# The opening of a two-layer encoder: the first quarter's scale and shift split into two eighths, the first weight items run chunk by chunk

## The chip, the cores and the metric

The kernel runs on one core of one Trainium2 chip. The metric is the device time in microseconds; lower is better. Engines are TensorE (PE, its weight loads PEld), VectorE (DVE), ScalarE (ACT), GpSimd (POOL) and SyncE (SP), whose queue issues nearly all DMAs.

## The reference, cut to what matters

```python
def hybrid_layer(x, c, ...):
    mod = jax.nn.silu(c) @ ada_w + ada_b                      # 1024 -> 6 x 1024
    sh_m, sc_m, g_m, sh_f, sc_f, g_f = jnp.split(mod, 6)
    h = rms_norm(x, norm_mix_g) * (1 + sc_m) + sh_m           # 256 tokens x 1024
    proj = h @ w_in
    ...                                                       # three attention branches, merge, FFN
```

Two such layers follow one another, then a last RMSNorm. All is float32. At the start of the program `h` of layer 0 needs two of the six modulation vectors, the shift `sh_m` and the scale `sc_m`; each is a row of 1024 numbers, a product of the vector silu(c) with a 1024 x 1024 matrix.

## The kernel before, in words

Tokens are two tiles of 128 (t = 0, 1). The model width of 1024 is eight chunks of 128 (kc = 0 to 7). A float32 product is made of three passes in a faster format: an operand is split into a rounded part (`hi`, by a cast on ACT) and the remainder (`lo`, by a subtraction on DVE), and the products are hi x hi, lo(weight) x hi and hi(weight) x lo.

Weights come in items of up to 256 rows x 512 columns, that is two chunks of the contraction. `load_split` (L242 to L254) loads an item into `raw`, casts it into `whi` (L189) and makes `wlo` (L190). The function `mm` of an item (L263 to L272) issues for one token tile the three passes over its two chunks: 6 matmuls, so 12 for both tiles. An item's eight-chunk sum takes four items.

The first 12 items belong to three groups of columns (416, 512 and 512 wide) whose items are interleaved, so that items 0, 1 and 2 need only chunks 0 and 1 of `h`, items 3, 4, 5 chunks 2 and 3, and so on. Item 2 is loaded in two DMAs, items 0 and 1 in one. Accordingly the scale and shift are made in four quarters of 256 columns each (two chunks):

- `first_loads(q)` (L861) issues the quarter's 8 DMAs of 256 KB, rows of 256 numbers. Nothing but SP's order and a limit of 8 DMAs in flight holds them up.
- `first_sums(q)` (L877) multiplies them with silu(c) on PE (L883, a 32-column weight), 8 matmuls of 512 columns, and ACT copies the sums out (L886).
- `first_mod(q)` (L889) transposes them on PE (L892), DVE reduces them (L894), and `first_apply` (L898) makes scale and shift (L902, L905, L903), then the two chunks of `h`: `hi` on ACT (L910), the full value on DVE (L911) and `lo` (L915).

The main loop (L929 on) writes the order of PE by hand for the opening: 16 warm-up matmuls (L842), the transposes of the normalised x (`first_x`), the first quarter, then item 0; the sums of the next quarter before the second of three items, its transposes before the third. The order of SP's queue is that of the code: the columns of parameters, x, the constants (`con`, L83: rotary tables, mask and the 128 x 128 identity that transposes need, which is its last 128 columns), the first quarter, items 0 and 1, the second quarter, item 2 and so on. The parameters at item 7 (L320 to L334), and what comes behind, read the rest of the constants.

Of the kernel before, what the change touches and what calls it, by code (L numbers as in the profile page):

```python
# [36 lines left out]
def encoder_kernel(ctx: ExitStack, tc: tile.TileContext, x, consts, cols, rows, ada_b, rpb, ada_w, w_in,  # L37
                   w_uq, w_ukv, w_na, w_mla, w_gqa, w_out, w_gu, w_dn, fng, out):
    nc = tc.nc
# [30 lines left out]

    def tpb():
        return pstp.tile([P, 512], F32, tag="tp", name=nm("tp"))
# [41 lines left out]
    mods = {}  # L114
# [121 lines left out]
    items = []  # L236
    state = {}

    def add(srcs, nk, n, mm, post=None, pre=()):
        items.append(dict(srcs=srcs, nk=nk, n=n, mm=mm, post=post, pre=list(pre)))  # L240
        return items[-1]

    def load_split(it):
        nk, n = it["nk"], it["n"]
        raw = rawp.tile([P, 2, 512], F32, tag="raw", name=nm("raw"))
        c = 0
        for src in it["srcs"]:
            w = src.shape[1]
            nc.sync.dma_start(raw[:, 0:nk, c:c + w], src.rearrange("(k p) n -> p k n", p=P))
            c += w  # L250
        hi = spl.tile([P, 2, 512], F32R, tag="whi", name=nm("whi"))
        lo = spl.tile([P, 2, 512], F32R, tag="wlo", name=nm("wlo"))
        split_to(hi[:, 0:nk, 0:n], lo[:, 0:nk, 0:n], raw[:, 0:nk, 0:n])
        it["w"] = (hi, lo)  # L254

    def group(units_src, nkc, n, lhs, post, bank=None):

        ps = {}
        nu = (nkc + 1) // 2
# [27 lines left out]
    cur = [0]  # L287
# [545 lines left out]
    xT0 = {}  # L833
# [5 lines left out]
    def warm(n):  # L839

        for _ in range(n):
            nc.tensor.matmul(warm_ps, warm_w[:, 0:P], warm_w, start=True, stop=True)  # L842

    def last_pe():
        return next(i for i in reversed(nc.cur_bb.bb.instructions) if i.engine == mybir.EngineType.PE)

    def first_x():
        xT = act.tile([P, KC, S], F32, tag="lo", name=nm("xT"))
        for hf in range(2):
            xT0[hf] = xT[:, hf * 4:hf * 4 + 4, :]  # L850
        for t in range(NT):
            for hf in range(2):
                sumsq(t, hf, ss0[t])
            r = x_rstd(t, ss0[t])
            for hf in range(2):
                nc.scalar.copy(xT0[hf][:, :, t * P:(t + 1) * P], transposed(x_scaled(t, r, hf)))
        state[0]["hT"] = act_tiles()
        mods[(0, 1)] = modp.tile([P, KC], F32, tag="c1", name=nm("cm"))
        mods[(0, 0)] = modp.tile([P, KC], F32, tag="c0", name=nm("cm"))

    def first_loads(q):  # L861

        raws = []
        for v in range(4):
            raw = t4([P, 2, 2, 256])
            for mi, m in enumerate((1, 0)):
                c0 = m * D + q * 256
                nc.sync.dma_start(raw[:, :, mi, :], ada_w[0, v * 256:(v + 1) * 256, c0:c0 + 256].rearrange(
                    "(k p) n -> p k n", p=P))
            raws.append(raw.rearrange("p k m n -> p k (m n)"))  # L870
# [6 lines left out]
    def first_sums(q, raws):  # L877


        ps = tpb()  # L880
        for kc in range(KC):
            j = kc % 4
            nc.tensor.matmul(ps[32 * j:32 * j + 32, :], scz[:, kc, :], raws[kc // 2][:, kc % 2, :], start=(kc < 4),  # L883
                             stop=(kc >= 4), tile_position=(0, 32 * j))
        four = t2([P, 512])
        nc.scalar.copy(four, ps)  # L886
        return four

    def first_mod(q, four):  # L889
        pv = tpb().rearrange("p (j q) -> p j q", j=4)  # L890
        for j in range(4):
            nc.tensor.transpose(pv[:, j, :], four[:, j * P:(j + 1) * P], ident)  # L892
        red = sm(4)
        nc.vector.tensor_reduce(out=red, in_=pv.rearrange("p j (r z) -> p j r z", z=32)[:, :, :, 0], op=ALU.add, axis=AX.X)  # L894
        with tc.high_priority():
            first_apply(q, red)

    def first_apply(q, red):  # L898
        k0 = 2 * q
        A, B, hT = mods[(0, 1)], mods[(0, 0)], state[0]["hT"]  # L900
        r2 = sm(2)
        nc.vector.tensor_tensor(out=r2, in0=red[:, 0:2], in1=colp(0, "b", KC + k0, 2), op=ALU.add)  # L902
        nc.vector.scalar_tensor_tensor(out=A[:, k0:k0 + 2], in0=r2, scalar=1.0, in1=colp(0, "gm", k0, 2), op0=ALU.add,  # L903
                                       op1=ALU.mult)
        nc.vector.tensor_tensor(out=B[:, k0:k0 + 2], in0=red[:, 2:4], in1=colp(0, "b", k0, 2), op=ALU.add)  # L905
        full = t2([P, 2, S])
        for j in range(2):
            kc = k0 + j
            xv = xT0[q // 2][:, kc % 4, :]
            nc.scalar.activation(hT[0][:, kc, :], xv, AF.Identity, scale=A[:, kc:kc + 1], bias=B[:, kc:kc + 1])  # L910
            nc.vector.tensor_scalar(out=full[:, j, :], in0=xv, scalar1=A[:, kc:kc + 1], scalar2=B[:, kc:kc + 1],  # L911
                                    op0=ALU.mult, op1=ALU.add)
        for j in range(2):
            kc = k0 + j
            nc.vector.tensor_tensor(out=hT[1][:, kc, :], in0=full[:, j, :], in1=hT[0][:, kc, :].bitcast(F32),  # L915
                                    op=ALU.subtract)

    def run_mm(t, i):
        it = items[i]
# [4 lines left out]
    def step(t, i):  # L924
        run_due(cur[0])
        run_mm(t, i)
        cur[0] += 1

    pend = []  # L929
    for i, it in enumerate(items):  # L930
        if i in flush:
            while pend:
                step(1, pend.pop(0))
        if i == 0:
            raws = first_loads(0)
            with tc.manual_schedule(engines={mybir.EngineType.PE}):
                warm(16)
                first_x()
                four = first_sums(0, raws)
                warm(1)  # L940
                first_mod(0, four)
                warm(1)
        for f in side.get(i, ()):
            f()
        load_split(it)
        if i < 12:

            q1 = i // 3 + 1
            if i % 3 == 1 and q1 < 4:
                raws = first_loads(q1)  # L950
            with tc.issue_after(last_pe()), tc.manual_schedule(engines={mybir.EngineType.PE}):
                if i % 3 == 1 and q1 < 4:
                    four = first_sums(q1, raws)
                if i % 3 == 2 and q1 < 4:
                    first_mod(q1, four)
# [78 lines left out]
```

## Time and profile before

| | |
|---|---|
| median of 3 runs | 815.99 us (815.93 to 816.52) |
| the profiled execution | 816.62 us |
| its span, first to last instruction | 814.7 us |
| mean granted TensorE clock | 0.997 of full speed |
| busy | PE 97%, DVE 74%, ACT 56%, POOL 3% |
| DMA | 187 MB, mean 230 GB/s |

Times in the profile count from the first instruction. A matmul's busy time overlaps that of the next, since matmuls are pipelined; how far apart two of them start tells more. "Idle before" an instruction is time in which its engine did nothing, with the instruction that ended the wait. For a DMA the profile tells when SP issued it and how long after that it had landed.

### The profile page before, as it was taken

How to read it: one execution, taken by the hardware profiler on the slowest of the kernel's cores; microseconds unless marked ns; L12 is line 12 of the kernel's file. 1: busy time of each engine (PE TensorE's matmuls, PEld its weight loads, DVE VectorE, ACT ScalarE, POOL GpSimd, SP SyncE). 2: the span in 40 equal slices, each digit the busy share in tenths (PEclk: the TensorE clock that was granted, in tenths of full speed). 3: DMA queues.
4: the chain of work that ended last, by engine and by line, in shares of the span. 5: the costliest groups of instructions: out<-in, count | busy, mean ns of one | idle time of the engine just before them, and what ended most of it. 6: DMA issues, size and time to landing. Idle time of an engine off the chain costs nothing.

```text
span 814.7 us, 10812 instructions
## 1 busy us (share of the span) xinstructions
PE 791.9 (97%) x3778; PEld 630.9 (77%) x3778; DVE 599.2 (74%) x961; ACT 454.1 (56%) x788; POOL 24.6 (3%) x40
## 2 busy tenths in 40 slices
PE   7999999999999999999989999999999999999996
PEld 4677677788878878888878877777887888888884
DVE  3469899889777888865576798878987676665562
ACT  4465978645484444454466797764548544444441
POOL 1001000000000000000000020000000000000000
PEclk9999999999999999999999999999999999999998
DMA  9987598795548888875865568768765677765521
GB/s 313 360 281 202 169 308 280 259 312 192 192 159 293 292 284 318 275 261 185 206 191 173 173 192 281 231 220 294 229 205 181 222 243 223 255 219 182 183 102 52
DMA packets 113414, 187.20 MB, mean 230 GB/s; under 512 B 14672, under 2 KB 34256, under 8 KB 113360
## 3 DMA queue, kind: packets, MB, share of 16 engines
q1 hardware_dynamic: 113360, 186.51, 71.4%
q8 instruction: 30, 0.49, 0.2%
q14 instruction: 24, 0.20, 0.1%
HBM read 185.44 MB, written 1.05 MB: 229 GB/s over the span
## 4 chain that ended last, share of the span: by engine, by line
issue 49%; PE 31%; DVE 7%; ACT 6%; DMA 5%; POOL 1%; SPq 0%; POOLq 0%; DVEq 0%; ACTq 0%
PE mm L271 24%; DVE wlo L190 3%; DMA raw<-in_ada_w_dram 2%; PE tp L569 2%; DMA raw<-in_w_mla_dram 2%; DVE acc L142 1%; PE o L638 1%; ACT P L596 1%; PE tp L617 1%; ACT whi L189 1%; PE tp L883 1%; ACT tm L220 1%; DMA con<-in_consts_dram 1%; DMA s<-in_ada_w_dram 1%; ACT P L601 1%
## 5 line engine op out<-in xcount | busy, mean ns | idle before, releaser
L189 ACT CAST whi<-raw 128x1024 fp32r<-128x1024 f32 (+2 forms) x248 | 257.0, 1042 | 229.5 <-PE mm L271 141.1
L190 DVE TENSOR_TENSOR wlo<-raw,whi 128x1024 fp32r<-128x1024 f32 (+2 forms) x248 | 297.7, 1207 | 112.9 <-ACT whi L189 112.4
L271 PE MATMUL mm<-whi,hi 128*128 128x512 f32 (+1 forms) x784 | 249.8, 399 | 1.9 <-ACT hi L910 1.1
L271 PE MATMUL mm<-wlo,hi 128*128 128x512 f32 (+1 forms) x784 | 242.9, 391 | 1.2 <-DVE wlo L190 1.1
L271 PE MATMUL mm<-whi,lo 128*128 128x512 f32 (+1 forms) x784 | 242.2, 390 | 0.6 <-DVE lo L915 0.6
L271 PEld LDWEIGHTS mm<-whi,lo 128*128 128x128 f32 x784 | 147.1, 188 | 33.7 <-DVE lo L915 1.6
L271 PEld LDWEIGHTS mm<-wlo,hi 128*128 128x128 f32 x784 | 146.5, 188 | 32.4 <-DVE wlo L190 2.3
L271 PEld LDWEIGHTS mm<-whi,hi 128*128 128x128 f32 x784 | 141.1, 188 | 34.0 <-issue 6.0
L142 DVE SCALAR_TENSOR_TENSOR acc<-raw,sc,acc 128x512 f32<-128x512 f32 x140 | 104.6, 747 | 28.1 <-DMA raw<-in_ada_w_dram 26.4
L271 PE MATMUL mm<-whi,s 128*128 128x512 f32 (+1 forms) x376 | 104.6, 390 | 0.0
L271 PEld LDWEIGHTS mm<-whi,s 128*128 128x128 f32 x376 | 69.8, 188 | 14.1 <-issue 0.3
L271 PE MATMUL mm<-wlo,s 128*128 128x512 f32 (+1 forms) x188 | 58.2, 388 | 0.0
L271 PEld LDWEIGHTS mm<-wlo,s 128*128 128x128 f32 x188 | 35.2, 188 | 7.1
L601 ACT ACTIVATE P<-P,sm 128x256 f32<-128x256 f32 x64 | 29.2, 509 | 2.8 <-DVE sm L599 2.8
L596 ACT ACTIVATE P<-tp,sm,rq 128x256 f32<-128x256 f32 x32 | 17.8, 563 | 12.5 <-DVE sm L593 12.5
L220 ACT ACTIVATE tm<-tp,cm,cm 128x128 f32<-128x128 f32 x48 | 21.3, 471 | 5.9 <-PE tp L211 5.9
L199 POOL TENSOR_SCALAR sm<-ss 128x1 f32<-128x1 f32 x10 | 4.0, 397 | 659.4 <-ACT tm L194 659.4
L110 POOL TENSOR_TENSOR sm<-sm,nhalf 128x1 f32<-128x1 f32 (+2 forms) x22 | 18.4, 835 | 125.5 <-DVE sm L380 63.1
L194 ACT ACTIVATE tm<-x_sb 128x512 f32<-128x512 f32 x20 | 12.6, 632 | 16.8 <-DVE x_sb L713 14.6
L743 DVE TENSOR_TENSOR tm<-tm,mm 128x512 f32<-128x512 f32 (+1 forms) x24 | 15.3, 638 | 8.6 <-PE mm L271 7.0
L543 ACT ACTIVATE s<-mm 128x512 f32<-128x512 f32 x24 | 14.3, 595 | 9.9 <-PE mm L271 9.9
L617 PE MATMUL tp<-con,P 128*128 128x128 f32 x128 | 19.0, 276 | 0.3 <-DVE G L177 0.3
(160 smaller groups left out, 603.7 us busy)
## 6 DMA issues: line engine op xcount, KB each, us to landing
raw<-in_ada_w_dram SPq DMA_DIRECT2D x80, 512.0 KB, 4.7
raw<-in_w_gu_dram SPq DMA_DIRECT2D x80, 512.0 KB, 4.3
raw<-in_w_in_dram SPq DMA_DIRECT2D x64, 512.0 KB, 4.7
raw<-in_w_dn_dram SPq DMA_DIRECT2D x44, 512.0 KB, 4.6
s<-in_ada_w_dram SPq DMA_DIRECT2D x32, 256.0 KB, 6.8
raw<-in_w_out_dram SPq DMA_DIRECT2D x16, 512.0 KB, 4.7
raw<-in_w_in_dram SPq DMA_DIRECT2D x16, 256.0 KB, 4.8
raw<-in_w_gqa_dram SPq DMA_DIRECT2D x8, 512.0 KB, 5.8
```

The source lines that it names most:

```text
L110: nc.gpsimd.tensor_tensor(out=r, in0=ms, in1=nhalf[:, 0:n], op=ALU.pow)
L142: nc.vector.scalar_tensor_tensor(out=acc, in0=raw[:, j, :], scalar=sc[:, kc:kc + 1], in1=acc, op0=ALU.mult, op1=ALU.add)
L189: nc.scalar.copy(hi_ap, src)
L190: nc.vector.tensor_tensor(out=lo_ap, in0=src, in1=hi_ap.bitcast(F32), op=ALU.subtract)
L220: nc.scalar.activation(fv[:, j, :], xT[:, j, :], AF.Identity, scale=A[:, kc:kc + 1], bias=B[:, kc:kc + 1])
L271: nc.tensor.matmul(ps[t][:, 0:n], lhs(t, part, kc), w[:, j, 0:n], start=(kc == 0 and n_ == 0), stop=(kc == nkc - 1 and n_ == 2))
L543: nc.scalar.activation(st["gate"][gi][:, t, :], ps, AF.Tanh, scale=0.5)
L569: nc.tensor.matmul(sv[:, t, :], q(t), k, start=True, stop=True)
L596: nc.scalar.activation(pt[:, t, :], src[:, t, :], AF.Exp, bias=nb[:, t:t + 1], scale=scale[t], accum_out=rs[:, t:t + 1])
L601: nc.scalar.activation(pt[:, t, :], pt[:, t, :], AF.Copy, scale=rc[:, t:t + 1])
L617: nc.tensor.transpose(tv[:, k, t * P:(t + 1) * P], pts[i][:, t, k * P:(k + 1) * P], ident)
L743: nc.vector.tensor_tensor(out=hd[:, 0:n], in0=sgv, in1=up, op=ALU.mult)
```

## The change

The first quarter comes in two eighths of one chunk each (128 columns, so rows of 512 bytes; four DMAs of 256 KB for each). Of the constants only the identity is loaded ahead of them; the rest follows the second eighth. Items 0, 1 and 2 run their first chunk (`js=(0,)`) as soon as the first eighth is applied; then come the sums and the application of the second eighth, and then the second chunks of items 0, 1 and 2, with the sums of the second quarter behind item 0 and its transposes behind item 1.

```diff
-    nc.sync.dma_start(con, consts)
+    nc.sync.dma_start(con[:, NCON - P:NCON], consts[:, NCON - P:NCON])
...
-            def mm(t, it, u=u, nk=nk):
-                if u == 0:
+            def mm(t, it, u=u, nk=nk, js=None):
+                if u == 0 and t not in ps:
                     ps[t] = bank(t) if bank else psmm.tile([P, 512], F32, tag="mm", name=nm("mm"))
...
-                    for j in range(nk):
+                    for j in js or range(nk):
...
-    def first_loads(q):
+    def first_loads(k0, n):
 
         raws = []
-        for v in range(4):
-            raw = t4([P, 2, 2, 256])
+        nk = 4 // n
+        for v in range(KC // nk):
+            raw = t4([P, nk, 2, n * P])
             for mi, m in enumerate((1, 0)):
-                c0 = m * D + q * 256
-                nc.sync.dma_start(raw[:, :, mi, :], ada_w[0, v * 256:(v + 1) * 256, c0:c0 + 256].rearrange(
+                c0 = m * D + k0 * P
+                nc.sync.dma_start(raw[:, :, mi, :], ada_w[0, v * nk * P:(v + 1) * nk * P, c0:c0 + n * P].rearrange(
                     "(k p) n -> p k n", p=P))
...
         if i == 0:
-            raws = first_loads(0)
+            raws = first_loads(0, 1)
             with tc.manual_schedule(engines={mybir.EngineType.PE}):
                 warm(16)
                 first_x()
-                four = first_sums(0, raws)
+                four = first_sums(1, raws)
                 warm(1)
-                first_mod(0, four)
+                first_mod(0, 1, four)
                 warm(1)
...
-            if i % 3 == 1 and q1 < 4:
-                raws = first_loads(q1)
+            if i == 0:
+                raws = first_loads(1, 1)
+                nc.sync.dma_start(con[:, 0:NCON - P], consts[:, 0:NCON - P])
+            if i in (2, 4, 7):
+                raws_q = first_loads(2 * q1, 2)
             with tc.issue_after(last_pe()), tc.manual_schedule(engines={mybir.EngineType.PE}):
+                if i < 3:
+
+                    for t in range(NT):
+                        it["mm"](t, it, js=(0,))
+                    if i == 2:
+                        four = first_sums(1, raws)
+                        first_mod(1, 1, four)
+                        for k in range(3):
+                            if k == 1:
+                                four = first_sums(2, raws_q)
+                            if k == 2:
+                                first_mod(2, 2, four)
+                            for t in range(NT):
+                                items[k]["mm"](t, items[k], js=(1,))
+                    cur[0] += 2
+                    continue
```

`first_sums`, `first_mod` and what was `first_apply` do the same work for n = 1 or 2 chunks; in the changed kernel their lines are L886 (sums), L889 (copy), L895 (transposes) and L898 (reduction).

SP's queue, from the constants on. In the kernel before (`s` is a piece of a quarter, `raw` an item's weights; L868 is `first_loads`):

```order
L83 DMA con<-in_consts_dram 128x576
L868 DMA s_3_119<-in_ada_w_dram 128x2x256 x2
L868 DMA s_4_122<-in_ada_w_dram 128x2x256 x2
L868 DMA s_5_125<-in_ada_w_dram 128x2x256 x2
L868 DMA s_6_128<-in_ada_w_dram 128x2x256 x2
L249 DMA raw_234<-in_w_in_dram 128x2x416
L249 DMA raw_257<-in_w_in_dram 128x2x512
```

And in the changed one (L869 is `first_loads`):

```order
L83 DMA con<-in_consts_dram 128x128
L869 DMA s_3_119<-in_ada_w_dram 128x4x128 x2
L869 DMA s_4_122<-in_ada_w_dram 128x4x128 x2
L249 DMA raw_223<-in_w_in_dram 128x2x416
L869 DMA s_35_229<-in_ada_w_dram 128x4x128 x2
L869 DMA s_36_232<-in_ada_w_dram 128x4x128 x2
L951 DMA con<-in_consts_dram 128x448
L249 DMA raw_247<-in_w_in_dram 128x2x512
```

Item 0 (416 columns) has moved ahead of half of the first quarter; item 1 (512 columns) still has all of it, and all of the constants, ahead of it. Item 2 now comes right behind item 1, ahead of the second quarter.

PE behind the first warm-up and transposes. In the kernel before, from item 0 (`mm_242` and `mm_249` are its two token tiles) over the second quarter's sums to item 1 (`mm_288`):

```order
L271 MATMUL mm_242<-whi_236,hi_198 128x416 x2
L271 MATMUL mm_242<-wlo_237,hi_198 128x416 x2
L271 MATMUL mm_242<-whi_236,lo_199 128x416 x2
L271 MATMUL mm_249<-whi_236,hi_198 128x416 x2
L271 MATMUL mm_249<-wlo_237,hi_198 128x416 x2
L271 MATMUL mm_249<-whi_236,lo_199 128x416 x2
L883 MATMUL tp_277<-s_42_263,scz 32x512 x2
L883 MATMUL tp_277<-s_43_266,scz 32x512 x2
L883 MATMUL tp_277<-s_44_269,scz 32x512 x2
L883 MATMUL tp_277<-s_45_272,scz 32x512 x2
L271 MATMUL mm_288<-whi_259,hi_198 128x512 x2
```

In the changed kernel, from the end of item 2's first chunk (`tp_289` is its second tile) over the second eighth to the second chunk of item 0 (`mm_238`, `mm_242`):

```order
L271 MATMUL tp_289<-whi_267,hi_192 128x512
L271 MATMUL tp_289<-wlo_268,hi_192 128x512
L271 MATMUL tp_289<-whi_267,lo_193 128x512
L886 MATMUL tp_293<-s_35_229,scz 32x256 x4
L886 MATMUL tp_293<-s_36_232,scz 32x256 x4
L895 MATMUL tp_304<-con,tm_302 128x128 x2
L271 MATMUL mm_238<-whi_225,hi_192 128x416
L271 MATMUL mm_238<-wlo_226,hi_192 128x416
L271 MATMUL mm_238<-whi_225,lo_193 128x416
L271 MATMUL mm_242<-whi_225,hi_192 128x416
```

The second eighth's sums and transposes stand directly behind each other, with no product between them, and the product behind them is the first that reads what they lead to. From the sums of the third quarter on, the order of every engine is that of the kernel before.

## Rows read from the trace of the kernel before

**Rows 1.** The page's first line.

```profile
span 814.7 us, 10812 instructions
```

**Rows 2.** Busy time by stage: stretch, length, busy per engine (instructions), clock, DMA share, GB/s.

```profile
8.00:17.70 9.70, 7.27 (x38) 3.12 (x38) 2.06 (x9) 4.17 (x8) 0.66 (x2) 1.00 1.08 364
17.70:32.43 14.73, 14.34 (x68) 9.63 (x68) 7.97 (x16) 5.85 (x8) 0.00 (x0) 1.00 1.09 357
43.30:60.00 16.70, 16.50 (x84) 12.48 (x84) 10.82 (x20) 13.14 (x25) 1.40 (x2) 1.00 0.84 267
60.00:100.00 40.00, 39.27 (x198) 29.06 (x196) 36.56 (x97) 31.16 (x72) 5.56 (x6) 1.00 0.68 189
```

**Rows 3.** The chain of waits, 0 to 18 us: start, length, what.

```profile
2.10 5.88 DMA con<-in_consts_dram
...
15.69 0.67 PE tp L892 x4
...
16.39 0.19 DVE sm L894
...
17.05 0.61 ACT hi L910
```

**Rows 4.** Timeline 0 to 60 us: start, length, engine, line, operation, tiles, shapes, count, idle before.

```profile
17.05 1.09 ACT L910 ACTIVATE hi<-xT,cm,cm 128x256 fp32r<-128x256 f32 x2 [0.62 <-DVE cm L903]
...
17.70 0.94 PE L271 MATMUL mm<-whi,hi 128*128 128x416 f32 x2 [1.12 <-ACT hi L910]
...
18.05 1.03 ACT L189 CAST whi<-raw 128x1024 fp32r<-128x1024 f32 x1
...
18.65 0.75 DVE L915 TENSOR_TENSOR lo<-tm,hi 128x256 fp32r<-128x256 f32 x2
...
19.32 1.22 DVE L190 TENSOR_TENSOR wlo<-raw,whi 128x1024 fp32r<-128x1024 f32 x1
...
19.75 0.54 PE L271 MATMUL mm<-whi,hi 128*128 128x416 f32 x2
...
20.13 0.54 PE L271 MATMUL mm<-wlo,hi 128*128 128x416 f32 x2
...
23.42 0.73 PE L271 MATMUL mm<-whi,hi 128*128 128x512 f32 x2
...
26.28 0.60 PE L892 MATMUL tp<-con,tm 128*128 128x128 f32 x4
...
32.43 1.92 PE L883 MATMUL tp<-s,scz 128*32 128x512 f32 x16
```

**Rows 5.** Item 1's weights: SP's issue at 9.43, and the DMA's size and landing.

```profile
9.43 0.37 SPq L249 DMA_DIRECT2D raw<-in_w_in_dram  x1
...
raw<-in_w_in_dram SPq DMA_DIRECT2D x1, 512.0 KB, 6.8
```

**Rows 6.** A DMA with rows of 512 bytes and the one ahead: issues, then landings.

```profile
32.75 0.37 SPq L868 DMA_DIRECT2D s<-in_ada_w_dram  x1
33.49 0.34 SPq L323 DMA_DIRECT2D tm<-in_rows_dram  x1
...
s<-in_ada_w_dram SPq DMA_DIRECT2D x1, 256.0 KB, 6.6
...
tm<-in_rows_dram SPq DMA_DIRECT2D x1, 64.0 KB, 6.1
```

**Rows 7.** Stages again: the constants' first rows; the neighbourhood table's rows of 256 bytes.

```profile
5.25:6.75 1.50, 1.50 (x7) 0.90 (x5) 0.00 (x0) 1.44 (x7) 0.53 (x2) 1.00 0.89 244
64.10:68.00 3.90, 3.90 (x23) 3.25 (x22) 3.19 (x19) 1.67 (x5) 1.49 (x2) 1.00 1.17 189
```

**Rows 8.** Groups of ScalarE by shape: a copy of 256 columns; busy, mean ns.

```profile
L514 ACT COPY vb<-mm 128x256 f32<-128x256 f32 x4 | 1.5, 368 | 0.9 <-PE mm L271 0.9
```

**Rows 9.** Stages of the warm-up, all engines.

```profile
1.40:4.40 3.00, 2.96 (x7) 2.41 (x8) 0.43 (x2) 0.81 (x2) 0.00 (x0) 1.00 0.80 266
4.40:6.80 2.40, 2.36 (x10) 1.57 (x9) 0.00 (x0) 2.03 (x7) 0.57 (x2) 1.00 0.90 281
```

More of the change, by code (lines that the diff above doesn't have):

```diff
@@ L859, in first_x @@
         mods[(0, 0)] = modp.tile([P, KC], F32, tag="c0", name=nm("cm"))
-    def first_loads(q):
+    def first_loads(k0, n):
         raws = []
-        for v in range(4):
-            raw = t4([P, 2, 2, 256])
+        nk = 4 // n
+        for v in range(KC // nk):
+            raw = t4([P, nk, 2, n * P])
             for mi, m in enumerate((1, 0)):
-                c0 = m * D + q * 256
-                nc.sync.dma_start(raw[:, :, mi, :], ada_w[0, v * 256:(v + 1) * 256, c0:c0 + 256].rearrange(
+                c0 = m * D + k0 * P
+                nc.sync.dma_start(raw[:, :, mi, :], ada_w[0, v * nk * P:(v + 1) * nk * P, c0:c0 + n * P].rearrange(
                     "(k p) n -> p k n", p=P))
-            raws.append(raw.rearrange("p k m n -> p k (m n)"))
+            rv = raw.rearrange("p k m n -> p k (m n)")
+            raws += [rv[:, j, :] for j in range(nk)]
         return raws
@@ L875, in encoder_kernel, with first_sums @@
     nc.vector.tensor_copy(scz[:, :, 0], sc)
-    def first_sums(q, raws):
+    def first_sums(n, raws):
         ps = tpb()
+        w = 2 * n * P
         for kc in range(KC):
             j = kc % 4
-            nc.tensor.matmul(ps[32 * j:32 * j + 32, :], scz[:, kc, :], raws[kc // 2][:, kc % 2, :], start=(kc < 4),
+            nc.tensor.matmul(ps[32 * j:32 * j + 32, 0:w], scz[:, kc, :], raws[kc], start=(kc < 4),
                              stop=(kc >= 4), tile_position=(0, 32 * j))
         four = t2([P, 512])
-        nc.scalar.copy(four, ps)
+        nc.scalar.copy(four[:, 0:w], ps[:, 0:w])
@@ L887, in first_sums, with first_mod @@
         return four
-    def first_mod(q, four):
+    def first_mod(k0, n, four):
         pv = tpb().rearrange("p (j q) -> p j q", j=4)
-        for j in range(4):
+        for j in range(2 * n):
             nc.tensor.transpose(pv[:, j, :], four[:, j * P:(j + 1) * P], ident)
-        red = sm(4)
-        nc.vector.tensor_reduce(out=red, in_=pv.rearrange("p j (r z) -> p j r z", z=32)[:, :, :, 0], op=ALU.add, axis=AX.X)
         with tc.high_priority():
[L896 to L916, printed above, removed]
@@ new lines, in first_mod @@
+            red = sm(4)[:, 0:2 * n]
+            nc.vector.tensor_reduce(out=red, in_=pv.rearrange("p j (r z) -> p j r z", z=32)[:, 0:2 * n, :, 0],
+                                    op=ALU.add, axis=AX.X)
+            A, B, hT = mods[(0, 1)], mods[(0, 0)], state[0]["hT"]
+            r2 = sm(2)[:, 0:n]
+            nc.vector.tensor_tensor(out=r2, in0=red[:, 0:n], in1=colp(0, "b", KC + k0, n), op=ALU.add)
+            nc.vector.scalar_tensor_tensor(out=A[:, k0:k0 + n], in0=r2, scalar=1.0, in1=colp(0, "gm", k0, n),
+                                           op0=ALU.add, op1=ALU.mult)
@@ new lines, in first_mod @@
+            nc.vector.tensor_tensor(out=B[:, k0:k0 + n], in0=red[:, n:2 * n], in1=colp(0, "b", k0, n), op=ALU.add)
+            full = t2([P, 2, S])
+            for j in range(n):
+                kc = k0 + j
+                xv = xT0[kc // 4][:, kc % 4, :]
+                nc.scalar.activation(hT[0][:, kc, :], xv, AF.Identity, scale=A[:, kc:kc + 1], bias=B[:, kc:kc + 1])
+                nc.vector.tensor_scalar(out=full[:, j, :], in0=xv, scalar1=A[:, kc:kc + 1], scalar2=B[:, kc:kc + 1],
+                                        op0=ALU.mult, op1=ALU.add)
@@ L918, in run_mm @@
+            for j in range(n):
+                kc = k0 + j
+                nc.vector.tensor_tensor(out=hT[1][:, kc, :], in0=full[:, j, :], in1=hT[0][:, kc, :].bitcast(F32),
+                                        op=ALU.subtract)
     def run_mm(t, i):
@@ L948, in encoder_kernel @@
             q1 = i // 3 + 1
-            if i % 3 == 1 and q1 < 4:
-                raws = first_loads(q1)
-            with tc.issue_after(last_pe()), tc.manual_schedule(engines={mybir.EngineType.PE}):
+            if i == 0:
[3 more added lines that the diff above has]
+                raws_q = first_loads(2 * q1, 2)
+            with tc.issue_after(last_pe()), tc.manual_schedule(engines={mybir.EngineType.PE}):
+                if i < 3:
[13 more added lines that the diff above has]
+                    continue
                 if i % 3 == 1 and q1 < 4:
-                    four = first_sums(q1, raws)
+                    four = first_sums(2, raws_q)
                 if i % 3 == 2 and q1 < 4:
-                    first_mod(q1, four)
+                    first_mod(2 * q1, 2, four)
                 step(0, i)
```

## The prediction, made before the changed kernel ran

> **What bounds the kernel now.** I read the busy time by stage first [rows 1, 2]: between 17.70 and 32.43 us TensorE is busy 14.34 of 14.73 us, then 16.50 of 16.70 us (to 60 us; the stretch between is like the first) and 39.27 of 40.00 (to 100 us). From its first product on TensorE runs almost without a gap, so a microsecond by which the opening holds it up or lets it go early stays in the result, unless a wait takes it back. The same rows show the DMA engines at 364 and 357 GB/s until 32 us: what lands when is set there by the bytes that stand ahead in SP's queue, and 256 KB take 0.73 us.
>
> Next the chain of waits up to the first product [rows 3]: the DMA of the constants (issued at 2.10, landed 5.88 later), then the last piece of the first quarter, then one chain through all engines: transposes, reduction (16.39), scale and shift into hi (17.05). The timeline [rows 4] has the first product at 17.70, after 1.12 us of idle TensorE; the matmuls of items 0 to 2 are then packed, with the sums of the second quarter between them, and the sums of the third quarter start at 32.43. That row is my mark: behind it the two programs issue the same instructions in the same order on every engine. The change is worth what it moves that mark by.
>
> **The change, part by part.** Bytes first. Before, 288 + 2048 + 416 KB stand between x and the weights of item 1. Now it is 64 (identity) + 1024 (first eighth) + 416 + 1024 (second eighth) + 224 (rest of the constants): the same 2752 KB. What moves ahead is item 0 and its eighth; item 1 gains nothing. Its weights landed at 9.43 + 6.8 = 16.23 [rows 5]. But the two eighths come in rows of 512 bytes, where the quarter had 1024. The trace has one such DMA: 64 KB of the parameters, which landed at 33.49 + 6.1 = 39.59, the DMA ahead of it at 32.75 + 6.6 = 39.35 [rows 6]: about 0.2 us, so 0.8 for 256 KB. It reads one source row over and over, so it may flatter. From the other side, rows of 256 bytes move at 189 GB/s [rows 7], 1.39 us for 256 KB; the straight line in the number of rows from 0.73 (256 rows) to 1.39 (1024) gives 0.95 for 512. I take 0.87, between these two: the one has the same row size, the other a source row for each destination row. Eight such DMAs cost 8 x (0.87 - 0.73) = 1.1 us, and item 1 lands at 17.35. The bounds are 0.73 (16.23) and 1.39 (21.5). The Trainium skill (DMA: Bandwidth & Descriptors, Specifications) puts the least transfer for line rate at 512 B; by that the rows are free and the sum below is 1.1 lower.
>
> SP itself is no limit: it takes 0.37 us for an issue [rows 5], under the 0.73 of a landing. The rest of the constants is passed by nothing that reads it soon; its readers are the parameters at item 7 and later.
>
> The head start. Item 0 lands 512 KB (1.47 us), 224 KB (0.64) and an eighth (3.48) ahead of item 1, at 11.75. Its cast now stands on ScalarE ahead of the copy of the sums, and its low half on VectorE ahead of the reduction; by 832 of the 1024 columns of rows 4 these take 0.84 and 1.0. With 0.66 from reduction to hi and 0.65 from hi to the first product [rows 3, 4], that product starts near 15.0, some 2.7 us earlier. It has six matmuls to do and is finished by 16.6.
>
> Then it is spent. TensorE's next work is item 1, by the new order, and the second eighth, long landed, is behind items 1 and 2:
> - item 1: landed 17.35, cast 1.03, low half 1.22 [rows 4]: the second matmul can start at 19.7. Five more at 0.24 (12 in 26.28 - 23.42) end at 20.9.
> - item 2: 512 KB later, 18.8; cast to 19.85, low half behind item 1's to 21.1; five matmuls, 22.35. TensorE has by now idled about 3.2 us for items 1 and 2.
> - second eighth: sums of 256 columns, half of the 1.92 of rows 4 or 1.0, to 23.35; copy 0.37 [rows 8] to 23.75; two transposes, of the 0.67 for four [rows 3] about 0.45, to 24.2; 0.66 to hi at 24.9; first product 25.5, and its third matmul waits for lo (0.6 + 0.42 behind hi) until 25.95; four more at 0.19 end at 26.7. Before, all of this chain was paid once, ahead of the first product; now its second run of 2.15 us stands inside the stream, with nothing else for TensorE to do, and the 1.0 of sums with it.
> - second quarter: landed by 18.8 + 2048 KB at 357 GB/s = 24.7, not late; sums 1.9 to 28.6, half of item 1 (1.43) to 30.0, transposes 0.4, half of item 2 to 31.85.
> - item 3: transposes at 30.0, reduction 0.70 and hi 1.36 later, the second hi 1.09 after that: its second matmul starts at 32.55, eleven at 0.19 end at 34.65.
>
> The sums of the third quarter then start at 34.65 and not at 32.43: **2.2 us later**. Their data is there (24.7 + 928 KB + 2048 KB = 33.2 for the last piece, which is used last). The profiled execution took 816.62 us and its span 814.7 [rows 1], 0.63 over the median of the runs; the difference of 2.2 goes on either: 815.99 + 2.2 = **818.2**.
>
> **Rivals.** (1) Not slower. The eighths' rows move as fast as the quarter's did. Then item 1 lands at 16.23, all the rest follows, and the time is 817.1; if the slow stretch while the constants' first rows came in (244 GB/s [rows 7], the 288 KB landing 1.1 us late by the rate) goes with the smaller DMA too, 816.0. The point that decides is item 1's landing at 16.75: earlier than that, the loss is under 0.2%, or 1.63 us, which is what a measurement here can tell from no change. For it: the 64 KB DMA at 0.2 us. The rule of the Trainium skill (DMA: Bandwidth & Descriptors, Specifications) on 512 B says the same. Against it: that DMA had a single source row, and the slow stretch may come with any first touch of the constants.
>
> (2) Much slower: the short rows are read as slowly as those of 256 bytes. Item 1 then lands at 21.5, and the time is 818.2 + 4.2 = 822.4. Against it: 0.2 us for 64 KB.
>
> (3) The clock falls. TensorE has gaps of 1.9, 1.0 and 2.1 us between 16.6 and 25.5. Before, the idle 1.12 us ahead of 17.70 did not lower it: matmuls of 416 columns then follow at 0.19 [rows 4], and the granted clock is 1.00 [rows 2]. The price is in the warm-up: 3.0 us with 7 matmuls, then 2.4 us with 10 [rows 9], where they follow at half the rate and then at the full one; 3 us at the lower level, 1.2 GHz, lose about 1.5, and the time is 819.7. The Trainium skill (TensorE: Matmul & The Clock Gate, Part 1: The HAM clock gate) has an idle engine fall to 1.2 GHz; the longest gap here is about twice one that the trace shows harmless.
>
> (4) Faster by over 1.63 us. With all data there at once, item 1's cast would still follow hi of item 0 (14.35 + 0.6 by the numbers above), its low half would be there at 17.2, 2.5 us earlier than reckoned, and the time 815.7. No row gives more; the chance is for what I overlook.
>
> That the change isn't what it says can be left out: the new order has the split DMAs, and the wait for the rest of the constants is on a free DMA slot alone.
>
> **How the numbers follow.** Forecast, 817.6 to 820.4: 0.58. Rival 1: 0.31. Rivals 2 and 3: 0.04 each. Rival 4: 0.03. So slower 0.66, same 0.31, faster 0.03. The forecast's own range is 817.6 to 820.4, and by the straight line alone (0.95) it would be 818.8. For 8 in 10 I take in most of rival 1, without its last third, and leave the two dear cases out: 816.5 to 820.4.
>
> **What would show it.** Right: the first product near 15.0; a landing of item 1's weights near 17.3; idle TensorE ahead of items 1 and 2 of some 3 us, and again 2 us between the sums of the second eighth and the second half of item 0; the sums of the third quarter near 34.6; the same distance at every later row. Wrong: item 1 landed before 16.75, or a distance of 2 us at 34 us that is smaller at 100 us, which would mean that TensorE is not what bounds the stages in between; or a first product that is not earlier, if the copy of the first sums waits for item 0's cast longer than I reckon.

## The result, and the profile after

The changed kernel takes **821.56 us** (median of 5 runs, 819.11 to 822.21), the kernel before 815.93 (815.43 to 816.52): a ratio of 1.0062 (95% interval 1.0049 to 1.0074). It is slower by 5.1 us by the ratio, more than the 2.2 forecast, and outside the range. The profiled execution took 822.17 us.

The page's first line of the changed kernel [rows 1]:

```profile
span 820.1 us, 10848 instructions
```

Its busy time by the stages of [rows 2] (the clock is the column before the last two):

```profile
8.00:17.70 9.70, 6.34 (x41) 4.03 (x39) 3.19 (x10) 4.76 (x8) 0.74 (x2) 0.84 1.13 332
17.70:32.43 14.73, 12.24 (x52) 6.48 (x52) 5.98 (x10) 3.92 (x6) 0.00 (x0) 0.64 1.10 357
43.30:60.00 16.70, 16.49 (x87) 12.41 (x86) 12.13 (x34) 9.09 (x15) 0.00 (x0) 1.00 0.68 202
60.00:100.00 40.00, 39.27 (x194) 30.05 (x194) 35.38 (x95) 31.14 (x74) 6.96 (x8) 1.00 0.69 189
```

Two columns tell the difference. Between 17.70 and 32.43 us TensorE is busy 12.24 of 14.73 us where it was busy 14.34, and the granted clock is 0.64 where it was 1.00. From 43.3 us on TensorE is as busy as before. The same view, cut where the clock changes:

```profile
9.00:14.59 5.59, 3.33 (x29) 1.92 (x30) 2.75 (x9) 3.27 (x6) 0.00 (x0) 1.00 1.15 318
14.59:24.83 10.24, 8.66 (x26) 5.74 (x30) 2.74 (x3) 2.09 (x2) 0.00 (x0) 0.50 1.09 361
24.83:28.25 3.42, 1.64 (x19) 0.64 (x9) 1.36 (x6) 1.50 (x3) 0.00 (x0) 1.00 1.08 360
28.25:31.66 3.41, 3.41 (x17) 1.57 (x20) 2.17 (x2) 1.19 (x2) 0.00 (x0) 0.50 1.10 348
31.66:38.74 7.08, 7.05 (x40) 4.84 (x32) 2.03 (x8) 1.68 (x3) 0.00 (x0) 1.00 1.08 365
```

For 13.65 us of the opening TensorE runs at 1.2 GHz instead of 2.4. Its timeline, next to [rows 4]:

```profile
14.47 0.63 PE L271 MATMUL mm<-whi,hi 128*128 128x416 f32 x1 [1.27 <-ACT hi L910]
14.90 0.55 PE L271 MATMUL mm<-wlo,hi 128*128 128x416 f32 x1
15.24 0.55 PE L271 MATMUL mm<-whi,lo 128*128 128x416 f32 x1
...
17.94 0.79 PE L271 MATMUL mm<-whi,hi 128*128 128x512 f32 x1 [1.11 <-ACT whi L189]
19.20 0.79 PE L271 MATMUL mm<-wlo,hi 128*128 128x512 f32 x1 [0.47 <-DVE wlo L190]
...
24.19 1.36 PE L886 MATMUL tp<-s,scz 128*32 128x256 f32 x16
26.05 0.44 PE L895 MATMUL tp<-con,tm 128*128 128x128 f32 x2 [0.50 <-ACT tm L889]
27.77 0.46 PE L271 MATMUL mm<-whi,hi 128*128 128x416 f32 x1 [1.28 <-ACT hi L910]
...
38.74 0.64 PE L886 MATMUL tp<-s,scz 128*32 128x512 f32 x4
```

The starts show the forecast's mechanism: a first product 3.2 us earlier (14.47 for 17.70), idle time, then the second eighth's chain inside the stream. Both gaps, ahead of 17.94 and 19.20, are item 1's, for its rounded and its low half; item 2 followed without one. But 14.90 and 15.24 are 0.34 us apart where matmuls of 416 columns followed at 0.19. The mark, the sums of the third quarter, is at 38.74 and was at 32.43: 6.3 us later, not 2.2.

The distance does not stay at that. By the fourth quarter's sums it is 5.8 us (49.13 here, 43.30 before). The texts ahead say that from the mark on every engine has the order of before; there is one exception. VectorE makes the low half of item 6's weights ahead of the third quarter's reduction here (from 42.36 and at 44.44 us), and behind it before (37.87 and 37.78), so `lo` is ready in time here and was not before. Before:

```profile
41.45 0.79 PE L271 MATMUL mm<-whi,lo 128*128 128x416 f32 x2 [0.18 <-DVE lo L915]
```

and in the changed kernel:

```profile
47.41 0.66 PE L271 MATMUL mm<-whi,lo 128*128 128x416 f32 x2
...
49.13 1.92 PE L886 MATMUL tp<-s,scz 128*32 128x512 f32 x16
```

At 100 us it is still 5.8 (ScalarE's copy L622 at 104.62, before at 98.78). Behind that, single executions drift: 6.2 us at 226 us, 4.5 at 300, 5.4 at the end. So a profile's distances are read up to 100 us here, and whole times by the ratio.

The chain of waits from SP's issue of item 1 (landing 11.21 + 5.61 = 16.82) to the second chunk:

```profile
11.21 5.61 DMA raw<-in_w_in_dram
16.84 1.05 ACT whi L189
17.92 1.24 DVE wlo L190
...
19.20 2.50 PE mm L271 x5
21.70 1.28 PE o L271 x3
22.98 1.28 PE tp L271 x3
```

Behind item 1's landing and its two casts, eleven matmuls take 5.06 us; at 0.24 they would take 2.6.

### The profile page after: what moved, and what is told of

It reads as the page before. It is cut to its first block, busy times and chain, and to the rows that moved or that the text cites. A ratio compares the mean times of both kernels' runs of the same rounds, so it can differ in the third digit from the quotient of the medians.

```text
span 820.1 us, 10848 instructions
## 1 busy us (share of the span) xinstructions
PE 795.3 (97%) x3794; PEld 634.0 (77%) x3794; DVE 601.0 (73%) x965; ACT 454.0 (55%) x789; POOL 24.7 (3%) x40
## 4 chain that ended last, share of the span: by engine, by line
issue 47%; PE 39%; ACT 5%; DVE 4%; DMA 2%; SPq 1%; POOL 1%; POOLq 0%; DVEq 0%; ACTq 0%
PE mm L271 31%; PE tp L569 2%; PE o L638 2%; DMA raw<-in_ada_w_dram 1%; PE tp L617 1%; DVE wlo L190 1%; ACT P L596 1%; PE tp L886 1%; ACT tm L220 1%; DMA raw<-in_w_in_dram 1%; SPq L869 1%; POOL sm L110 1%; PE tp L271 1%; PE o L271 1%; ACT whi L189 1%
## 5 line engine op out<-in xcount | busy, mean ns | idle before, releaser
L760 ACT ACTIVATE tm<-mm 128x512 f32<-128x512 f32 x20 | 11.9, 596 | 13.9 <-PE mm L271 13.2
```

## The experiments

Each was timed beside runs of the kernel before on the same chip (medians 815.85 to 816.46 there); the ratio is what compares them. Two theories stood at the start. A: most of what the forecast missed is the clock. B: the reordered opening itself costs more than was reckoned.

**1. Fillers everywhere.** Warm-up matmuls into columns that nobody reads, in all gaps of the opening.

```diff
-                warm(1)
+                warm(4)
                 first_mod(0, 1, four)
-                warm(1)
+                warm(6)
...
+                    if i == 1:
+                        warm(8)
```

and 3 and 9 fillers of 256 columns behind the second eighth's sums and behind its transposes, in the same banks.

> The changed kernel with idle TensorE filled by matmuls on zeros whose results nobody reads: 3 + 5 more in the first eighth's chain, 8 ahead of item 1, 3 + 9 of 256 columns in the second eighth's chain. Theory A (the clock): in the changed kernel the granted clock stood at half from 14.6 to 24.8 us and from 28.2 to 31.7, and that made about 4 of the 5.6 us; the rest is the wait for items 1 and 2 and the second chain. Then the clock stays at 1.00 here, the sums of the third quarter start near 34.2 us (changed kernel 38.7, kernel before 32.4), and the time is 817.6 (816.9 to 818.3). Theory B (data alone): the matmuls of that stretch wait for weights at either clock. Then the time stays over 820 though the clock holds.

Measured: 818.93 us, ratio 1.0032 (1.0021 to 1.0044); in the profile the clock is 1.00 throughout the opening, the mark at 36.21. Half of the loss went with the clock. But the fillers cost something themselves. TensorE's fillers behind the transposes, and the first product after them:

```profile
24.21 1.32 PE L881 MATMUL tp<-warm_w 128*128 128x256 f32 x9
26.80 0.46 PE L271 MATMUL mm<-whi,hi 128*128 128x416 f32 x1 [1.28 <-ACT hi L917]
```

and VectorE's reduction, which by its row waited for them and not for the transposes at 24.01:

```profile
25.56 0.17 DVE L905 TENSOR_REDUCE sm<-tp 128x2 f32<-128x8 f32 x1 [5.02 <-PE tp L881]
```

**2. Fillers in the first chain alone** (`warm(4)`, `warm(6)`, nothing at item 1 or later).

> The changed kernel with the added matmuls on zeros in the first eighth's chain alone (3 + 5 more, ahead of 14.5 us). Theory A: if the idle time ahead of 14.6 us set off the fall, the first low stretch goes or comes later and shorter, and the time lies between 817.6 and 820; if the waits for items 1 and 2 set it off, the low stretch moves to about 18 to 28 us and the time stays at 820 to 822. Theory B: 821 to 822 whatever the clock does.

Measured: 821.7 us, ratio 1.0071 (1.0048 to 1.0095), as slow as the change. In the profile the clock held through the first product and fell at the next gaps, and the mark is at 36.41. This profiled execution (820.37 us, mean clock 0.996) is one of the better ones: three of the other five have a mean clock of 0.990 to 0.992.

```profile
8.00:19.51 11.51, 8.07 (x52) 5.26 (x52) 4.83 (x12) 5.89 (x9) 1.02 (x2) 1.00 1.13 335
19.51:22.93 3.42, 3.42 (x9) 2.68 (x10) 1.22 (x1) 0.10 (x1) 0.00 (x0) 0.50 1.10 348
```

Ahead of 19.51 TensorE had idled 1.98 and 0.76 us for item 1's two halves.

**5. Fillers that nobody waits for.** As 1, but the fillers of the second eighth stand ahead of its transposes, and behind them in the bank that the second quarter's sums overwrite.

```diff
+                        ps2 = tpb()
+                        fill(8, ps2[:, 0:256])
...
-                                four = first_sums(2, raws_q)
+                                four = first_sums(2, raws_q, ps2)
```

> The changed kernel with the same fillers as the first experiment, but the ones in the second eighth's chain go into columns that no waiting instruction reads (ahead of the transposes in their own bank, and in the bank of the next quarter's sums). Theory A (with the clock kept, only the chain of the second eighth in the stream is left, and 1.07 us of the first experiment's loss came from its own fillers, behind which the reduction waited): the granted clock is 1.00 from 5 to 800 us, the first product of the second chunk comes at about 25.7 us and not at 26.80, the sums of the third quarter at about 35.1 and not at 36.21, and the time is 2.5 us over the kernel before taken beside it, about 818. Theory B (the fillers cost nothing there, and the first experiment showed the whole price of the structure): sums at 36.2, 3.6 us over in the trace, about 819.

Measured: 817.84 us, ratio 1.0028 (1.0018 to 1.0039). Its clock, at the changed kernel's first low stretch:

```profile
14.59:24.83 10.24, 9.32 (x56) 6.58 (x56) 3.38 (x8) 2.51 (x4) 0.00 (x0) 1.00 1.10 361
```

and its timeline of TensorE:

```profile
14.54 0.46 PE L271 MATMUL mm<-whi,hi 128*128 128x416 f32 x1
...
19.28 0.50 PE L271 MATMUL mm<-wlo,hi 128*128 128x512 f32 x1 [0.77 <-DVE wlo L190]
...
22.15 1.07 PE L890 MATMUL tp<-s,scz 128*32 128x256 f32 x16
...
25.44 0.46 PE L271 MATMUL mm<-whi,hi 128*128 128x416 f32 x1 [0.33 <-ACT hi L916]
...
34.85 1.07 PE L890 MATMUL tp<-s,scz 128*32 128x512 f32 x8
```

VectorE and ScalarE run the changed kernel's order here; only fillers differ. So the clock is worth 1.0062 - 1.0028, or 2.8 us, by the ratios (1.4 to 4.1 with both intervals), and the reordered opening at full clock the 2.3 that is left (1.5 to 3.2). The two profiled executions say 3.9 at the mark and 3.8 at 100 us (the copy L622 stands at 100.78 here, 2.0 behind before).

**9. The later fillers alone** (as 5, with `warm(1)` and `warm(1)` in the first chain).

> The fifth experiment without its extra fillers in the first chain (4 and 6 products there are 1 and 1 again, as in the changed kernel); the fillers ahead of item 1 and in the second eighth's chain stay. Theory A (two falls of the clock with two causes: the sparse work ahead of the first product and the gaps at items 1 and 2): the clock falls at about 14.6 us as in the changed kernel, since the work ahead of it is the same, comes back within 3.4 us or 10 us, and does not fall again; sums of the third quarter between 35.5 and 37, time between those of the fifth experiment and the changed kernel, 818.5 to 820.5. Rival (one cause only, the gaps at items 1 and 2 and the second eighth): full rate throughout, sums at 34.9, time as in the fifth experiment, 817.8.

Measured: 818.25 us, ratio 1.0025 (1.0014 to 1.0035); full rate throughout the opening in the profile, mark at 35.09. At the changed kernel's first low stretch:

```profile
14.59:24.83 10.24, 9.11 (x54) 6.38 (x54) 3.23 (x6) 2.59 (x4) 0.00 (x0) 1.00 1.09 358
```

The rival held: fillers at item 1 and in the second eighth together are enough, those in the first chain neither enough (2) nor needed. Which of the two later places decides was not taken apart.

**7. The kernel before with a sparser first chain** (both `warm(1)` taken out).

```diff
                 four = first_sums(0, raws)
-                warm(1)
                 first_mod(0, four)
-                warm(1)
```

> The kernel before without the two single warm-up products in the first quarter's chain (one ahead of the transposes, one behind them); nothing else differs, and no wait hangs on them. Theory A (it is the sparse work ahead of the first product that lowers the granted clock): the clock falls to half at some point between 14 and 22 us, matmuls of 512 columns in the stream then stand 0.43 us apart for 3 to 10 us, and the time is 1.7 to 5 us over the kernel before: 818 to 821. Theory B (the gaps behind the first product, at items 1 and 2, are what lowered it in the changed kernel): the clock stays at full rate and the time is that of the kernel before within 0.5 us, 816.4.

Measured: 815.74 us, ratio 0.9998 (0.9989 to 1.0007). Theory A was half right: in the profile the clock is at half from 17.20 to 20.61 us, but the time is that of before.

```profile
17.18 1.21 PE L271 MATMUL mm<-whi,hi 128*128 128x416 f32 x2 [1.35 <-ACT hi L910]
18.27 1.06 PE L271 MATMUL mm<-wlo,hi 128*128 128x416 f32 x2
...
21.40 1.92 PE L883 MATMUL tp<-s,scz 128*32 128x512 f32 x16
23.26 0.73 PE L271 MATMUL mm<-whi,hi 128*128 128x512 f32 x2
```

The first product is 0.52 us early, and not because two matmuls less stand in the chain: from the start of the last sums to it take 3.73 us (13.45 to 17.18), before 3.74. The landings were early in this execution. The constants, the same 288 KB in the same place, were in at 7.42 us, before at 7.97 [rows 3]:

```profile
2.10 5.32 DMA con<-in_consts_dram
```

The sums of the second quarter start 0.42 us late (20.98 before). They end early all the same: before they spread over 2.44 us, waiting for pieces; the product at 23.26 stood at 23.42 [rows 4]. From the first product to the mark (32.28) it takes 15.10 us, before 14.73. So of the 1.7 us of work that 3.41 us at half rate hold up (an estimate from these two numbers) 0.37 are left at the mark: a fall costs less where a DMA and not TensorE ends the wait. The equal times alone do not show that: the mean clocks of the executions run from 0.994 to 0.998 here and in the kernel before beside it, so that kernel may have such falls too in executions that were not profiled. (The means also take in the program's end, where the clock of every profile here is at half, so they do not say where a fall was.)

**3. The identity alone.** The kernel before, with only the identity ahead of the first quarter and the rest of the constants behind the second quarter.

```diff
-    nc.sync.dma_start(con, consts)
+    nc.sync.dma_start(con[:, NCON - P:NCON], consts[:, NCON - P:NCON])
...
+                if i == 1:
+                    nc.sync.dma_start(con[:, 0:NCON - P], consts[:, 0:NCON - P])
```

> The kernel before with one part of the change: of the constants only the identity ahead of the first quarter, the rest behind the second quarter. Quarters, rows of 1 KB and the order on TensorE are those of before. In the changed kernel the identity landed at 6.4 us (the whole constants at 8.0 before), so the first quarter should land at 12.4 and not 13.8, the first product start near 16.3 (before 17.7), the sums of the third quarter near 31.0 (before 32.4), and the time be 814.5. Rival: the second quarter lands no earlier, its sums wait, and the time is 815.5 to 816.

Measured: 816.02 us, ratio 1.0001 (0.9989 to 1.0013): a miss. Its profiled execution ran at a granted clock of 0.85 throughout, so only its orders and waits are read. VectorE before:

```profile
25.09 1.23 DVE L190 TENSOR_TENSOR wlo<-raw,whi 128x1024 fp32r<-128x1024 f32 x1 [4.55 <-ACT whi L189]
26.92 0.17 DVE L894 TENSOR_REDUCE sm<-tp 128x4 f32<-128x16 f32 x1 [0.60 <-PE tp L892]
```

and in the experiment:

```profile
26.57 0.17 DVE L894 TENSOR_REDUCE sm<-tp 128x4 f32<-128x16 f32 x1 [6.64 <-PE tp L892]
26.68 1.23 DVE L190 TENSOR_TENSOR wlo<-raw,whi 128x1024 fp32r<-128x1024 f32 x1
```

The scheduler put the reduction ahead of item 2's low half, so that VectorE stood idle until the transposes while that item's `whi` was there, and TensorE then idled 0.93 us ahead of item 2's second product.

**6. The identity alone, order kept.** The rest of the constants at `i == 4`; every engine but SP then has the order of before.

> The kernel before with only the identity of the constants ahead of the first quarter, the rest of them issued behind the third quarter's pieces (i of 4), so that the order on VectorE and ScalarE is that of the kernel before. Theory A (the third experiment's gain was lost because VectorE took the second quarter's reduction ahead of the low half of item 2's weights): no idle 0.9 us ahead of item 2's second product, first product about 17.0 and not 17.70, sums of the third quarter about 31.8 and not 32.43, time 0.6 to 0.7 us under the kernel before. Rival (the 224 KB that go behind return the time elsewhere, since the same bytes are needed by 43 us): same time as before within 0.3 us.

Measured: 815.41 us, ratio 0.9996 (0.9987 to 1.0005). The idle 0.93 us is gone, the first product at 16.54. But the constants stood behind item 4 and still ahead of the third quarter, not behind it as the expectation says, and the mark's gain did not last:

```profile
31.27 2.60 PE L883 MATMUL tp<-s,scz 128*32 128x512 f32 x16
33.80 0.73 PE L271 MATMUL mm<-whi,hi 128*128 128x512 f32 x2
```

The sums start 1.16 us earlier than before but take 2.5, since the quarter's last piece lands at 32.68, as before (32.69). The times of 3 and 6 cannot be told apart (0.9989 to 1.0013, and 0.9987 to 1.0005), so that the swap cost time is not shown.

**11. The rest of the constants truly behind the third quarter**, and **12.** the same with `warm(2)` and `warm(5)` in the first chain.

```diff
             if i % 3 == 1 and q1 < 4:
                 raws = first_loads(q1)
+                if i == 4:
+                    nc.sync.dma_start(con[:, 0:NCON - P], consts[:, 0:NCON - P])
```

> The sixth experiment with the rest of the constants truly behind the third quarter's pieces (there it stood behind item 4 but still ahead of that quarter). Theory A (in the sixth experiment the sums of the third quarter started 1.16 us earlier, but their last piece landed at 32.68 as in the kernel before, so that only 0.49 us were left): the last piece lands at about 32.1, the sums take 2.0 us and not 2.5, the product behind them starts at about 33.4 and not 33.80 (34.29 in the kernel before), and the time is 0.7 to 0.9 us under the kernel before. Rival (something else held those sums, or a later landing takes the rest): 0.5 us under it or less, as in the sixth.

> The eleventh experiment with 2 and 5 warm-up products in the first quarter's chain instead of 1 and 1; they stand in the idle 0.24 us ahead of the transposes and the idle 1.12 us ahead of the first product. Theory A (in the eleventh's profile the clock was at half from 17.94 to 21.36 us, so that item 0's 12 matmuls took 4.64 us instead of 3.35; its executions with a mean clock of 0.997 or 0.998 have a median of 814.3, those with 0.996 one of 815.7): full rate throughout, item 0 in 3.4 us, sums of the third quarter at about 31.8 and not 32.67, median about 814.4, some 1.4 us under the kernel before. Rival (the fall costs nothing here, since the second quarter's pieces, landing until 21.83, hold the sums anyway): as the eleventh, 815.1.

Measured: 11 takes 815.15 us, ratio 0.9983 (0.9974 to 0.9993); 12 takes 815.27, ratio 0.9990 (0.9981 to 1.0000). 11 is **the best of these and faster than both kernels**, by 0.17% and as the lowest of twelve ratios, though not by theory A's way: in its profile the last piece landed at 32.72, and the mark was at 32.67, after a low clock from 17.94 to 21.36. In 12 the clock held and the mark came at 31.33, 1.1 us early; it was no faster than 11 by the ratios. What caps 12 is further on. The fourth quarter's sums and the product behind them, before:

```profile
43.30 1.92 PE L883 MATMUL tp<-s,scz 128*32 128x512 f32 x16
45.16 0.73 PE L271 MATMUL mm<-whi,hi 128*128 128x512 f32 x2
```

and in experiment 12:

```profile
42.27 2.18 PE L883 MATMUL tp<-s,scz 128*32 128x512 f32 x16
44.39 0.73 PE L271 MATMUL mm<-whi,hi 128*128 128x512 f32 x2
```

The last piece of that quarter lands at 43.36 in 12 and at 43.35 before: the same bytes stand ahead of it. Of 1.03 us at the start of the sums 0.77 are left behind them.

**4, 8, 10. The change, ordered better.** The second eighth's sums and application go right behind item 0's first chunk, then come item 0's second chunk and items 1 and 2 whole, with fillers.

```diff
+                if i == 0:
+                    for t in range(NT):
+                        it["mm"](t, it, js=(0,))
+                    four = first_sums(1, raws)
+                    warm(3)
+                    first_mod(1, 1, four)
+                    warm(6)
+                    for t in range(NT):
+                        it["mm"](t, it, js=(1,))
+                if i == 1:
+                    for t in range(NT):
+                        it["mm"](t, it)
```

> The changed kernel with the second eighth's sums and application right behind item 0's first chunk, then item 0's second chunk and items 1 and 2 whole; added matmuls on zeros in both chains; all DMAs in the changed kernel's order. If the place of the second chain behind items 1 and 2 is what costs, beside the clock, the sums of the third quarter start near 33.1 and the time is 816.6; by the order the casts of items 1 and 2 stand ahead of the second eighth's steps on ScalarE and VectorE, so it doesn't get under 816. If the short rows and the added sums cost, wherever they stand, it is 818 like the filled one.

In 8 the casts of items 1 and 2 are issued behind that chain, in one hand-ordered block with it:

```diff
-                    warm(3)
+                    warm(1)
                     first_mod(1, 1, four)
-                    warm(6)
+                    warm(4)
+                    load_split(items[1])
+                    load_split(items[2])
```

and in 10 item 4's likewise behind `first_mod(2, 2, four)`. In 8 the rest of the constants stands ahead of the third quarter, as in 6.

> The fourth experiment (second eighth's sums, transposes and values right behind item 0's first chunk, then item 0's second chunk, items 1 and 2 whole) with three things put right: the rest of the constants goes behind the third quarter's pieces (item 1 lands about 0.6 us earlier), ScalarE copies the second eighth's sums ahead of casting item 1, VectorE reduces them ahead of the low halves of items 1 and 2, and fewer fillers stand in the chain (1 and 4). Theory A (the fourth experiment lost its time on those orders: 0.78 us of copy behind a cast, 0.74 us of the second chunk's low half behind item 2's): first product of the second chunk about 19.5 and not 20.61, sums of the third quarter about 32.5 and not 34.45, time that of the kernel before within 0.7 us, about 816.5. Rival (the second quarter's pieces, landing until about 24.7, and the chain behind them hold the stream): sums at 33.5 or later, 817.3 or more.

> The eighth experiment with the second quarter's scale and shift made on VectorE ahead of item 4's low half (it stood 1.13 us behind it there, and TensorE idled 0.99 us for it), and with the rest of the constants truly behind the third quarter's pieces. Theory A (the idle 0.99 us goes, and the sums of the third quarter then wait for nothing): sums of the third quarter at about 32.2 and not 33.17, time about 0.6 us under the eighth experiment, 815.8 against 816.3 for the kernel before. Rival (the bytes bound it: the third quarter's last piece lands at about 33.2, so the sums end near 33.5 at the earliest): the same start, but the matmuls behind the sums at 34.1 or later, and the time that of the kernel before within 0.4 us.

Measured: 4 takes 817.45 us, ratio 1.0019 (1.0008 to 1.0030); 8 takes 816.49, ratio 1.0005 (0.9993 to 1.0016); 10 takes 816.80, ratio 1.0012 (1.0002 to 1.0021). In 8 the second chunk starts at 19.40 (19.5 expected) but the mark is at 33.17, not 32.5: VectorE put item 4's low half into the second quarter's chain, and TensorE idled 0.99 us. In 10 that idle is gone and the mark at 32.14, but 0.96 us of the same kind came back at 39.18, ahead of an item's second product. So the split, with the clock held and the second chain put where TensorE waits for item 1 anyway, comes level with the kernel before in 8 and beats it nowhere.

## Why the prediction was wrong

The direction and the waits of the sum were right; the clock was left out of the sum, and with it went the time. Step by step:

| | forecast | change | experiment 5 |
|---|---|---|---|
| first product | 15.0 | 14.47 | 14.54 |
| item 1, second matmul | 19.7 | 19.20 | 19.28 |
| sums of the second eighth | 22.35 | 24.19 | 22.15 |
| first product of the second chunk | 25.5 | 27.77 | 25.44 |
| sums of the third quarter | 34.65 | 38.74 | 34.85 |
| time, us | 818.2 | 821.56 | 817.84 |

- **The bytes.** Item 1 landed at 16.82, not 17.35. The rows of 512 bytes cost what was reckoned: the first eighth's pieces land from 7.5 to 10.2 us, 0.89 apart (0.87 forecast, 0.73 with rows of 1024). The rule of the Trainium skill (DMA: Bandwidth & Descriptors, Specifications), by which 512 B would be free, does not hold here by 0.16 us per 256 KB. What was half a microsecond off is the slow stretch, which rival 1 named: x and the identity are in at 6.4 us, so that stretch is all but gone. That the smaller DMA did this is not shown: in experiment 7 the whole constants landed 0.55 us earlier than before with nothing changed ahead of them.
- **The structure.** At full clock every step of the sum is within 0.5 us of experiment 5 and the mark within 0.2. So "2.2 us later" was right as far as it went, and a little lucky: the steps began 0.42 us early, with item 1, and took 0.62 longer from there to the mark (15.57 us for 14.95).
- **The step that failed** is the spacing of the matmuls. The sum puts those of items 1 and 2 at 0.24 us and all behind them at full rate, so the clock's term in it is nothing; in the change the eleven of items 1 and 2 took 5.0 us. The clock stood beside the sum as rival 3, with a chance of 0.04 and a price of 1.5 us; it measured 2.8 by the ratios. The chance rested on the idle 1.12 us ahead of 17.70, which lowered nothing in one profiled execution. But one gap in front of a packed stream is not three gaps with single matmuls and short groups between them; experiments 2, 5 and 9 show that the gaps at item 1 and at the second eighth together decide. The price took one stretch of 3 us. (Its source, [rows 9], gives the clock as 1.00 in both stretches; that the first was at half rate is read from the spacing, 0.43 and 0.24 us.) The changed kernel had 13.65 us: against experiment 5, 2.1 us of it were paid in the eleven matmuls of items 1 and 2 (19.20 to 24.19 against 19.28 to 22.15), 0.3 in the second eighth's chain, 0.7 in item 0's second chunk and 0.8 in the second quarter's sums. The five executions had mean clocks of 0.990 to 0.996, the profiled one the lowest, so the price differs from one to the next. The Trainium skill (TensorE: Matmul & The Clock Gate, A second HAM failure mode: psum-queue depth-cycling) tells of another kernel, in which short idles between groups of matmuls made the clock go down and up again; the trace shows the same picture, at 14.59, 24.83, 28.25 and 31.66 us, with waits for weights and for the second eighth as the idles.
- **Rival 1** did not come: item 1's landing at 16.82 was just past the 16.75 named as deciding, and experiment 5, at full clock, is still slower by 0.28% (0.18 to 0.39%).
- **Rivals 2 and 4** did not come. That 821.56 lies near rival 2's 822.4 is chance: the pieces landed 0.89 apart, not 1.39. The gain of 4 was out of reach as long as the fourth quarter's last piece lands at 43.35, behind the mark (experiment 12).

Left open: in the changed kernel the clock had fallen at 14.59, ahead of the gaps at item 1, and in the profile of experiment 9 it had not, with the same first chain. Experiments 7 and 11 show a fall near 17 to 18 us in a kernel with the order of before, so such a fall may come in some executions and not in others; the mean clocks of experiment 9's executions, 0.996 to 0.998, do not rule out a short one in some of them. What sets off the first fall stays open. That the gaps then keep the clock low is argued from 2, 5 and 9; it was not seen apart.

## What to carry to other kernels

A head start is worth what the next operands let it keep: the change began 3.2 us earlier and had nothing to multiply, and what it bought with that was gaps, which cost the clock. When a change puts gaps into a packed stream of matmuls, reckon the matmuls between and behind the gaps at half rate too, and try fillers, in columns that no waiting instruction reads. And look for the landing that caps all gain before shaping an order: here the last piece at 43.35 us left 0.8 us to what experiment 12 won ahead of it.

## What the hardware showed that was not expected

- A reduction of other columns of a bank waited for fillers in that bank: it started 1.55 us behind its transposes (24.01 to 25.56), and 0.46 in experiment 5 (23.73 to 24.19). So the mark of experiment 1 (36.21 for 34.85) understates what the clock is worth; the two times cannot be told apart (ratios 1.0032 and 1.0028). That the wait goes by the tile, not by its columns, may be the compiler's doing.
- What a fall costs goes by the order. From the first product to the mark the kernel before takes 14.73 us and experiment 12 14.72, both at full clock; with 3.4 us at half it is 15.10 in experiment 7 and 15.47 in 11. In the changed order it is 20.31 at full clock (experiment 5; 20.32 in 9), 21.73 with 3.4 us at half (experiment 2) and 24.27 with 13.65.
- Moving one 224 KB load changed the order of two VectorE instructions 10 us later, and with it put 0.93 us of idle time into TensorE's stream (experiment 3). An experiment that is meant to move bytes alone has to keep every engine's order.
- Landings differ by half a microsecond between executions: with the same DMAs ahead of it, the first quarter's last piece was in at 13.33 us in experiment 11 and at 12.73 in 12, and the first product followed 3.87 and 3.88 us later. A single profile does not settle a gain of that size.
